# One run of products per adaLN unit, an earlier last pivot, and a buffer of its own for the gMLP gate

## The chip, the core and the metric

The kernel runs on one core of a Trainium2 chip. A core has a matrix engine (TensorE, called PE, whose weight loads are listed as PEld), a vector engine (DVE), a scalar engine (ACT), GpSimd (POOL) and a sync engine (SP) that here issues nearly all transfers, in order, to 16 DMA engines. Matrix products accumulate in PSUM, which has eight banks of 128 x 512 fp32; all else lies in SBUF. The metric is the device time of one execution in microseconds; the median of the runs is given.

## What is computed

One layer of a streaming encoder (D = 1024) is computed for two groups with the same weights: a prompt of 1024 frames and a sample of 32 rows, one for each of 32 running streams. Both have conditioning vectors `c`, from which adaLN makes six modulation vectors; three kinds of head groups share one input projection.

```python
mod = silu(c) @ w_ada + b_ada                       # 1024 -> 6 * 1024
sh1, sc1, g1, sh2, sc2, g2 = split(mod, 6)
h = x * (1 + sc1) + sh1
mq, mk, mv, mo, mi, mf, fq, fk, fv, ff, gu, gv = split(h @ w_in)
hm = mlstm(mq, mk, mv, li, lf) -> head norm * gain * sigmoid(mo)     # 4 heads of 64
hf = softmax(q k^T * scale + F_i - F_j, causal) v                    # FoX, 8 heads of 64
hg = gu * (w_s (causal, blocks of 128) @ layer_norm(gv) + b_s)       # gMLP, 4 groups of 64
x = layer_norm(ALPHA * x + (1 + g1) * (concat(hm, hf, hg) @ w_o))
h = x * (1 + sc2) + sh2
y = (silu(h @ w_gate) * (h @ w_up)) @ w_down                         # 2816 wide
x = layer_norm(ALPHA * x + (1 + g2) * y)
```

The outputs are both groups' `x` and their new caches (FoX keys, values and forget values, mLSTM states, and for the sample the normalised `gv`).

## The kernel before

**Precision and products.** Every large fp32 product is taken as three fp32r products: each operand is split in a high part (an ACT cast, name ending in `hi` or `h`) and the remainder (a subtraction on DVE or POOL, `lo` or `l`), and `gemm` issues high x high (L119), high x low (L120) and low x high (L121). `tm_unit`, whose result has frames on the partitions, does the same at L315 to L317. In all listings the name before `<-` is the result and those behind it are the operands.

**Columns.** Activations lie transposed, features on partitions. The 1056 columns are two parts: part 0 holds the first 512 frames, part 1 the rest and the sample's 32 columns. `MM[0]` cuts part 0 into two pieces of 256 columns, `MM[1]` part 1 into two of 272.

**Order.** The program is written as generators. A scheduler places each instruction on its engine's stream by a simulated timeline, by the priority of its place in the program, by dependences and by free buffers; `tc.high_priority(n)` moves what is written inside it ahead by n places. A buffer is named by pool and tag, and the last argument of `self.t` is how many copies rotate. Within an engine and on SP's queue everything runs in the order that results.

**The stages**, by the profile's times:

- 0 to 57 us: `x` is loaded, the eight adaLN units 0 to 7 (sh1, sc1) are computed, and the first feature-major projection `fm_first` runs as the operand's parts become ready.
- 57 to 150 us: values (`tm_unit` with `evac_v`) and gates.
- 150 to 370 us: the list `ORDER` says what comes in turn: `q`, `k`, `v`, `o` are projections, `f` is the first half of a FoX head, `m` an mLSTM head, and `a` one adaLN unit of the list `rest`. Results for the output projection go to DRAM (`start_dmix`).
- 370 to 408 us: gMLP. Four calls of `tm_unit` alternate between `evac_gv` (normalised `gv`, stored to DRAM as `start_dvn`) and `evac_gmlp` (the gate). `evac_gmlp` reads back `gvn` (L675), copies the gate `u` out of PSUM (L677), runs four small products with the spatial weights (L682), multiplies, and hands on to `to_mix`, which transposes, copies to a buffer `mixs` (L666) and stores it. Two feature-major units for heads 2 and 3 follow (`fm_g`, evacuated to `fm_qkh` at L399).
- 408 to 490 us: the output projection of part 0 (`wo`, products `wo_g`), its layer norm, four more feature-major units. Before `wo`, `wo_res` loads eight pieces of `x` (`mlstm_z<-xT`, a buffer that reuses the memory of the mLSTM heads) and `wo_mix` loads 16 pieces of the mixed heads (`wo_tmp<-start_dmix`, four buffers), which ACT casts (L947) and DVE subtracts (L948).
- 490 to 905 us: the second halves of the FoX heads and the other mLSTM heads are woven between the feed-forward part: six groups of hidden units (`GROUPS`), for each the `up` products (`up_g`, `L119` to `L121`, with the SiLU at L1058 to L1064) and then `down` (`dn_g`).
- 905 us to the end: the output projection and feed-forward of part 1 and the last layer norms.

**adaLN unit.** `ada(u)` makes 256 columns of the modulation: eight products of `c` (128 x 32 a slice) with 128 x 256 slices of `w_ada`. Each product has 32 result rows, placed by `k` in one of the four row quarters of a bank; the first four start the sums, the other four add to them. Then ACT copies the bank, PE transposes it (L196), DVE adds the four quarters (L198) and the bias (L204). Units 0 to 7 use the tag `araw`; the later 16 are called by `more(n)` with the tag `late`, in the PSUM tag `t`.

**Pivot.** The layer norm subtracts from every row block `z[:, m]` a common row, the mean of block `m = 0` (the pivot), before it sums squares. For part 0's last norm this stood in the fifth `down` group (`g == WOB - 1`): after `m = 0` one product with `ones8` (L891), an ACT copy (L892) and a DVE subtraction; then, for each `m` from 1, a POOL subtraction ahead of the DVE addition that evacuates the product:

```python
if pivot and m:
    self.nc.gpsimd.tensor_tensor(z[:, m, sl], z[:, m, sl], st["pv"][:, sl], ALU.subtract)   # L983
...
    self.lastz = self.nc.vector.scalar_tensor_tensor(z[:, m, x:y], ps[:, x - a:y - a], g[i], z[:, m, x:y],  # L986
```

The same stands for part 1 in its second-last `down` group. The functions as they were:

Of the kernel before, what the change touches and what calls it, by code (L numbers as in the profile page):

```python
# [15 lines left out]
P = 128  # L16
D = 1024
KT = 8
# [16 lines left out]
XB, AB = (3, 6)  # L35
HPA = 200
MLB = (1, 3, 5, 6, 7)
RESE = "pp"
ORDER = "q0 f0 q1 a f1 a q2 f2 k0 a k1p s a q3 f3 a v q4 f4 a a q5 f5 a o a m0 q6 f6 a m1 q7 a m2 f7 a m3"
ADAPOS = 4  # L40
# [27 lines left out]
class Kernel:  # L68
# [103 lines left out]
    def ada_load(self, u, pool, tag, bufs):  # L172
        self.phase = "ada"
        out = [self.t(pool, [P, 1056], F32, tag, bufs)[:, :1024] for _ in range(2)]
        for half, raw in enumerate(out):
            self.load(raw, self.d["w_ada"][u, :, half * 1024:(half + 1) * 1024])
        return out

    def ada(self, u, pool, tag, bufs, ppool, ptag, loaded=None):
        self.phase = "ada"  # L180
        nc = self.nc
        ps = self.t(ppool, [P, 512], F32, ptag)
        for half in range(2):
            if loaded:
                raw = loaded[half]
            else:
                raw = self.t(pool, [P, 1056], F32, tag, bufs)[:, :1024]
                self.load(raw, self.d["w_ada"][u, :, half * 1024:(half + 1) * 1024])
            for k in range(4):
                nc.tensor.matmul(ps[32 * k:32 * k + 32, :256], self.c32[:, 4 * half + k, :],  # L190
                                 raw[:, k * 256:(k + 1) * 256], start=half == 0, stop=half == 1)
# [113 lines left out]
    def tm_unit(self, src, ncol, evac, tiles=range(9), eng=None):  # L305
# [3 lines left out]
        for tt in tiles:  # L309
# [16 lines left out]
            else:  # L326
                tmp = self.t(self.sm, [NS, 264], F32, "tmsum", 1)
                nc.scalar.copy(tmp[:, :ncol], ps[32:64, :ncol])
                r = self.t(self.sm, [NS, 264], F32, "tmres", 1)
# [218 lines left out]
    def mlstm(self, j):  # L548
# [97 lines left out]
        sq = t([P, 4, 64], "msq")  # L646
# [25 lines left out]
    def evac_gmlp(self, tt, ps, n, bank=None):  # L672
# [3 lines left out]
        u = self.t(self.sm, [P, 256], F32, "traw", 2)  # L676
# [210 lines left out]
    def ln_pivot(self, st, z, sl):  # L887
        nc = self.nc
        ps = self.t(self.pt, [P, 512], F32, "t")
# [308 lines left out]

    def down(self, c, g, act, cuts, st=None, kept=None):
# [39 lines left out]
    def run(self):  # L1239
# [54 lines left out]
        rest = list(range(16, 20)) + list(range(8, 16)) + list(range(20, 24))  # L1294

        def more(n):
            for u in rest[:n]:
                self.ada(u, self.pl, "late", 2, self.pt, "t")
            del rest[:n]
# [49 lines left out]
        def tail_ada():  # L1349
            for u in rest:  # L1350
                self.ada(u, self.wp, "raw", RAW, self.pg, "g")

        for i in range(4):
            if i == ADAPOS:
                tail_ada()
            self.tm_unit(w2[3 + i % 2], 256, (self.evac_gv, self.evac_gmlp)[i % 2], range(4 * (i // 2), 4 + i // 2 * 5),
                         nc.gpsimd if GENG[i] else nc.vector)
        if ADAPOS == 4:
            tail_ada()
# [26 lines left out]
        for g, (j0, nj) in enumerate(GROUPS):  # L1386
# [52 lines left out]
        for g, (j0, nj) in enumerate(GROUPS):  # L1439
# [134 lines left out]
```

## Time and profile before

| what | value |
|---|---|
| median of 3 runs | 1422.57 us (1421.74 to 1427.48) |
| the profiled execution's own time | 1425.93 us |
| its span | 1424.1 us |
| mean granted TensorE clock | 0.986 |
| PE busy | 1354.6 us, 95% |
| DVE, ACT, POOL busy | 995.0, 653.3, 252.2 us |
| DMA | 233.06 MB, mean 164 GB/s |

Times in the views of the profile are microseconds from the span's start. A row of the timeline gives the start, the duration, the engine and line, the result and operands, and the shapes; a bracket behind it gives how long the engine sat idle before it and what ended that. A row of groups gives the shortest, median and longest duration in ns, and the first and last start. The granted clock is the share of TensorE's full clock that the chip gave. An fp32 product (as in `ada` and the transposes) makes two records.

### The profile page before, as it was taken

The page shows a single profiled execution, that of the slowest core. Times are in us where ns is not written, and L with a number is a line of the kernel's source. Part 1 is how long each engine was busy: PE and PEld are TensorE (multiplying, and loading weights), DVE is VectorE, ACT ScalarE, POOL GpSimd, SP SyncE. Part 2 cuts the span into 40 slices and gives each one's busy share as a digit, 9 for nine tenths or more (in the row PEclk, how much of TensorE's full clock was granted, in tenths as well). Part 3 has the DMA queues.
Part 4 walks back from the last instruction along what each step waited for, and adds up shares of the span by engine and source line. Part 5 has one row for each costly group of instructions (what it writes and reads, how often), then busy time and mean ns, then how long its engine had stood idle before and what let it go on. Part 6 is the DMA issues. An engine that isn't in the chain of part 4 may idle for free.

```text
span 1424.1 us, 25412 instructions
## 1 busy us (share of the span) xinstructions
PE 1354.6 (95%) x9435; PEld 1229.5 (86%) x9435; DVE 995.0 (70%) x2144; ACT 653.3 (46%) x1308; POOL 252.2 (18%) x290
## 2 busy tenths in 40 slices
PE   7999999899899899999999999999899999999995
PEld 4799888888899778888888877798899999999985
DVE  5548655558679757676767766577977888777766
ACT  3323244443444644545455354335654564636344
POOL 0103200032145700000000000274600000000431
PEclk9999999999999999999999999999999999999997
DMA  9764588677565464354445454555675768544221
GB/s 358 244 213 134 167 241 241 178 236 210 177 192 183 144 175 136 97 150 137 123 118 147 87 124 76 191 153 151 184 195 145 216 163 225 153 136 126 84 73 64
DMA packets 136371, 233.06 MB, mean 164 GB/s; under 512 B 22564, under 2 KB 79532, under 8 KB 136248
## 3 DMA queue, kind: packets, MB, share of 16 engines
q1 hardware_dynamic: 131080, 221.48, 51.4%
q0 software_dynamic: 5168, 9.96, 4.6%
q8 instruction: 74, 1.21, 0.3%
q14 instruction: 49, 0.40, 0.1%
HBM read 197.50 MB, written 53.81 MB: 176 GB/s over the span
## 4 chain that ended last, share of the span: by engine, by line
PE 79%; DMA 8%; DVE 7%; issue 2%; ACT 2%; POOL 1%; SPq 1%; ACTq 0%; DVEq 0%
PE up_g L119 5%; PE up_g L120 5%; PE up_g L121 5%; PE dn_g L119 4%; PE dn_g L120 4%; PE dn_g L121 4%; PE tm_g L316 3%; PE tm_g L315 3%; PE tm_g L317 3%; PE fm_g L119 2%; PE wo_g L121 2%; PE wo_g L120 2%; PE wo_g L119 2%; PE fm_g L120 2%; PE sup_g L119 2%
## 5 line engine op out<-in xcount | busy, mean ns | idle before, releaser
L119 PE MATMUL up_g<-mlstm_ah,up_whi 128*128 128x512 f32 x328 | 131.4, 401 | 2.5 <-DVE up_sil L1062 1.3
L120 PE MATMUL up_g<-mlstm_al,up_whi 128*128 128x512 f32 x328 | 130.4, 397 | 0.0
L121 PE MATMUL up_g<-mlstm_ah,up_wlo 128*128 128x512 f32 x328 | 129.8, 396 | 0.0
L315 PE MATMUL tm_g<-tm_whi,start_h1h 128*128 128x256 f32 (+1 forms) x384 | 111.4, 291 | 0.8 <-ACT tm_mixs L666 0.5
L316 PE MATMUL tm_g<-tm_wlo,start_h1h 128*128 128x256 f32 (+1 forms) x384 | 110.4, 288 | 0.0
L317 PE MATMUL tm_g<-tm_whi,start_h1l 128*128 128x256 f32 (+1 forms) x384 | 110.4, 288 | 0.0
L119 PE MATMUL fm_g<-start_h1h,fm_whi 128*128 128x256 f32 (+2 forms) x344 | 102.1, 303 | 8.2 <-DVE fm_qkl L400 5.1
L120 PE MATMUL fm_g<-start_h1l,fm_whi 128*128 128x256 f32 (+2 forms) x344 | 102.0, 297 | 0.0
L121 PE MATMUL fm_g<-start_h1h,fm_wlo 128*128 128x256 f32 (+2 forms) x344 | 101.3, 295 | 0.0
L1130 ACT CAST sup_whi<-sup_raw 128x1024 fp32r<-128x1024 f32 x54 | 56.5, 1048 | 80.9 <-PE dn_u L120 33.8
L107 ACT CAST up_whi<-up_raw 128x1024 fp32r<-128x1024 f32 x50 | 52.3, 1046 | 77.3 <-PE up_g L120 39.8
L751 ACT ACTIVATE fox_p<-fox_s,fox_fmx 128x384 f32<-128x384 f32 (+2 forms) x96 | 55.3, 580 | 59.6 <-DVE fox_fmx L744 52.7
L119 PE MATMUL dn_g<-up_acth,dn_whi 128*128 128x512 f32 (+2 forms) x200 | 75.1, 376 | 5.1 <-DVE mlstm_z L986 5.1
L782 DVE TENSOR_TENSOR fox_ptl<-fox_t,fox_pth 128x512 fp32r<-128x512 f32 (+2 forms) x88 | 51.0, 588 | 40.6 <-ACT fox_pth L781 40.1
L119 PEld LDWEIGHTS fm_g<-start_h1h,fm_whi 128*128 128x128 f32 x344 | 65.6, 192 | 14.4 <-DVE fm_qkl L400 6.0
L119 PEld LDWEIGHTS up_g<-mlstm_ah,up_whi 128*128 128x128 f32 x328 | 61.6, 188 | 17.4 <-DVE fm_qkl L400 1.8
L1131 DVE TENSOR_TENSOR sup_wlo<-sup_raw,sup_whi 128x1024 fp32r<-128x1024 f32 x54 | 67.5, 1256 | 13.0 <-ACT sup_whi L1130 12.8
L108 DVE TENSOR_TENSOR up_wlo<-up_raw,up_whi 128x1024 fp32r<-128x1024 f32 x50 | 62.2, 1244 | 19.8 <-ACT up_whi L107 19.2
L315 PEld LDWEIGHTS tm_g<-tm_whi,start_h1h 128*128 128x128 f32 x384 | 72.9, 190 | 3.1 <-issue 1.2
L316 PEld LDWEIGHTS tm_g<-tm_wlo,start_h1h 128*128 128x128 f32 x384 | 72.9, 190 | 1.9 <-issue 1.6
L120 PE MATMUL dn_g<-up_actl,dn_whi 128*128 128x512 f32 (+2 forms) x200 | 74.5, 373 | 0.0
L121 PE MATMUL dn_g<-up_acth,dn_wlo 128*128 128x512 f32 (+2 forms) x200 | 74.2, 372 | 0.0
(614 smaller groups left out, 4550.1 us busy)
## 6 DMA issues: line engine op xcount, KB each, us to landing
up_raw<-w_gu SPq DMA_DIRECT2D x50, 512.0 KB
ada_late<-w_ada SPq DMA_DIRECT2D x32, 512.0 KB
dn_raw<-w_dn SPq DMA_DIRECT2D x28, 512.0 KB
wo_raw<-w_o SPq DMA_DIRECT2D x24, 512.0 KB
sup_raw<-w_gu SPq DMA_DIRECT2D x20, 512.0 KB
start_dp<-w_gu SPq DMA_DIRECT2D x19, 512.0 KB
start_dp<-w_gu POOLq DMA_DIRECT2D x19, 512.0 KB, 6.9
sup_raw<-start_dp SPq DMA_DIRECT2D x18, 512.0 KB
```

Of the source, the lines that this page charges most:

```text
L107: nc.scalar.copy(hi[:, :w], raw[:, :w])
L108: (eng or nc.vector).tensor_tensor(lo[:, :w], raw[:, :w], f(hi[:, :w]), ALU.subtract)
L119: nc.tensor.matmul(ps, hi, xh(k), start=start and k == 0, stop=False, skip_group_check=more)
L120: nc.tensor.matmul(ps, hi, xl(k), start=False, stop=False, skip_group_check=more)
L121: nc.tensor.matmul(ps, lo, xh(k), start=False, stop=stop and k == n - 1, skip_group_check=more)
L315: nc.tensor.matmul(ps[:, :ncol], xh, hi, start=k == 0, stop=False)
L316: nc.tensor.matmul(ps[:, :ncol], xh, lo, start=False, stop=False)
L317: nc.tensor.matmul(ps[:, :ncol], xl, hi, start=False, stop=k == 7)
L751: nc.scalar.activation(pr[:, lo:hi], banks[x][:, :hi - lo], AF.Exp, bias=m, scale=-1.0 if hi == n else 1.0, accum_out=sums[:, x:x + 1])
L782: nc.vector.tensor_tensor(pl[:, :at], ps[:, :at], f(ph[:, :at]), ALU.subtract)
L1130: nc.scalar.copy(h, x)
L1131: tt(l, x, f(h), ALU.subtract)
```

## The change

Four edits. First, a unit's 1 MB of `w_ada` comes in one transfer, and its eight products are issued inside `high_priority(HPU)`; the copies of the buffers are half as many, each twice as large. Second, `ORDER` holds eight `a` instead of twelve: units 20 to 23 (the gate `g2`) are computed between the `up` units of part 0's feed-forward, in the PSUM tag `g` (three banks) of the `up` products, and `tail_ada`, which had nothing left to do, is gone. Third, a new `pivot(c)` does the whole subtraction, in pieces of 256 or 272 columns, after the fourth `down` group; the fifth has no pivot. Fourth, the gate `u` of `evac_gmlp` has two buffers `gu` of its own instead of sharing the two of `traw` with `evac_gv`; `msq` of the mLSTM head shares the buffers of `mkw`, and `tmres` is computed in place.

```diff
-XB, AB = (3, 6)
+XB, AB = (3, 3)
 HPA = 200
+HPU = 3000
-ORDER = "q0 f0 q1 a f1 a q2 f2 k0 a k1p s a q3 f3 a v q4 f4 a a q5 f5 a o a m0 q6 f6 a m1 q7 a m2 f7 a m3"
-ADAPOS = 4
+ORDER = "q0 f0 q1 a f1 a q2 f2 k0 k1p s a q3 f3 a v q4 f4 a q5 f5 o a m0 q6 f6 a m1 q7 m2 f7 a m3"
...
     def ada_load(self, u, pool, tag, bufs):
         self.phase = "ada"
-        out = [self.t(pool, [P, 1056], F32, tag, bufs)[:, :1024] for _ in range(2)]
-        for half, raw in enumerate(out):
-            self.load(raw, self.d["w_ada"][u, :, half * 1024:(half + 1) * 1024])
-        return out
+        raw = self.t(pool, [P, 2048], F32, tag, bufs)
+        self.load(raw, self.d["w_ada"][u])
+        return raw
...
         ps = self.t(ppool, [P, 512], F32, ptag)
-        for half in range(2):
-            if loaded:
-                raw = loaded[half]
-            else:
-                raw = self.t(pool, [P, 1056], F32, tag, bufs)[:, :1024]
-                self.load(raw, self.d["w_ada"][u, :, half * 1024:(half + 1) * 1024])
-            for k in range(4):
-                nc.tensor.matmul(ps[32 * k:32 * k + 32, :256], self.c32[:, 4 * half + k, :],
-                                 raw[:, k * 256:(k + 1) * 256], start=half == 0, stop=half == 1)
+        with self.tc.high_priority(HPU):
+            for k in range(KT):
+                r = slice(32 * (k % 4), 32 * (k % 4) + 32)
+                nc.tensor.matmul(ps[r, :256], self.c32[:, k, :], raw[:, k * 256:(k + 1) * 256],
+                                 start=k < 4, stop=k >= 4)
...
-                r = self.t(self.sm, [NS, 264], F32, "tmres", 1)
+                r = tmp
...
-        sq = t([P, 4, 64], "msq")
+        sq = t([P, 4, 64], "mkw")
...
-        u = self.t(self.sm, [P, 256], F32, "traw", 2)
+        u = self.t(self.sm, [P, 256], F32, "gu", 2)
...
-    def ln_pivot(self, st, z, sl):
+    def ln_pivot(self, st, z, sl, pool=None, tag="t"):
         nc = self.nc
-        ps = self.t(self.pt, [P, 512], F32, "t")
+        ps = self.t(pool or self.pt, [P, 512], F32, tag)
...
+    def pivot(self, c):
+        st = self.ln_begin(self.nc.gpsimd, early=True)
+        st["pivot"] = False
+        self.phase = f"dn{c}"
+        for a, b in MM[c]:
+            self.ln_pivot(st, self.z[c], slice(a, b), self.pg, "g")
+            for m in range(1, KT):
+                z = self.z[c][:, m, a:b]
+                st["eng"].tensor_tensor(z, z, st["pv"][:, a:b], ALU.subtract)
+        return st
...
-        rest = list(range(16, 20)) + list(range(8, 16)) + list(range(20, 24))
+        rest = list(range(16, 20)) + list(range(8, 16))
...
-                self.ada(u, self.pl, "late", 2, self.pt, "t")
+                self.ada(u, self.pl, "late", 1, self.pt, "t")
...
                 weave(self.up(0, j, act, pa, FC[0]))
-            if g == WOB - 1:
-                st = self.ln_begin(nc.gpsimd, early=True)
-                self.down(0, g, act, FC[0], st)
-            else:
-                self.down(0, g, act, FC[0])
-        st.update(pivot=False)
+                if j < 4:
+                    self.ada(20 + j, pa, "late", 1, self.pg, "g")
+            self.down(0, g, act, FC[0])
+            if g == WOB - 2:
+                st = self.pivot(0)
...
             if g < last:
-                st = self.ln_begin(nc.gpsimd, early=True) if g == last - 1 else None
-                self.down(1, g, act, MM[1], st)
-        st.update(pivot=False, order=(4, 5, 6, 7, 0, 1, 2, 3))
+                self.down(1, g, act, MM[1])
+            if g == last - 2:
+                st = self.pivot(1)
+        st.update(order=(4, 5, 6, 7, 0, 1, 2, 3))
```

The edits also change the scheduler's order. PE, in the head: before, the fourth adaLN unit of the head has its products in two pieces of four (`ada_t_328`); the numbers behind names tell buffers apart.

```order
L119 MATMUL fm_g_185<-start_h1h_168,fm_whi_248 128x512
L190 MATMUL ada_t_328<-ada_araw_323,start_c_63_181 32x256 x4
L120 MATMUL fm_g_186<-start_h1l_171,fm_whi_248 128x272
L121 MATMUL fm_g_186<-start_h1h_170,fm_wlo_249 128x272
L120 MATMUL fm_s_187<-start_h1l_171,fm_whi_248 128x272
```

After, the same unit (`ada_t_320`, the line is now L186) has them in one:

```order
L119 MATMUL fm_g_185<-start_h1h_168,fm_whi_244 128x512
L186 MATMUL ada_t_320<-ada_araw_316,start_c_63_181 32x256 x8
L120 MATMUL fm_g_186<-start_h1l_171,fm_whi_244 128x272
L121 MATMUL fm_g_186<-start_h1h_170,fm_wlo_245 128x272
L120 MATMUL fm_s_187<-start_h1l_171,fm_whi_244 128x272
```

All 24 units stand so: 24 pieces of eight, where before there were 40 pieces.

ACT, just before the output projection of part 0. Before, the casts of the mixed heads (L947) are spread among the gMLP copies (L666, L677) and the feature-major evacuations (L399):

```order
L947 CAST mlstm_ah_4416<-wo_tmp_4430 128x256
L666 COPY tm_mixs_5171<-tm_g_5132 128x256
L677 COPY tm_traw_5239<-tm_tmres_5235 32x256
L947 CAST mlstm_ah_4416<-wo_tmp_4434 128x256
L947 CAST mlstm_ah_4416<-wo_tmp_4438 128x256
L947 CAST mlstm_ah_4416<-wo_tmp_4442 128x256
L947 CAST mlstm_ah_4416<-wo_tmp_4446 128x256
L947 CAST mlstm_ah_4416<-wo_tmp_4450 128x256
L399 ACTIVATE fm_qkh_5285<-fm_g_5260,start_qsc_146 128x272
```

After, all gMLP copies come first (the gate's is now L673 and the mixed result's L662), and twelve of the sixteen casts (now L943) stand behind the last feature-major evacuation (now L395):

```order
L943 CAST mlstm_ah_4284<-wo_tmp_4298 128x256
L107 CAST wo_whi_5377<-wo_raw_5375 128x1024
L395 ACTIVATE fm_qkh_5260<-fm_g_5235,start_qsc_146 128x272
L943 CAST mlstm_ah_4284<-wo_tmp_4302 128x256
L943 CAST mlstm_ah_4284<-wo_tmp_4306 128x256
L943 CAST mlstm_ah_4284<-wo_tmp_4310 128x256
L943 CAST mlstm_ah_4284<-wo_tmp_4314 128x256
L943 CAST mlstm_ah_4284<-wo_tmp_4318 128x256
```

On SP the loads of `x` for part 0 (`mlstm_z<-xT`) stood ahead of the last gMLP stores; now they stand behind nearly all of them, and still behind the store of the last mLSTM head:

```order
L90 DMA start_dmix_32_88<-mlstm_mixs_4261 128x2x128
L90 DMA start_dmix_33_89<-tm_mixs_5038 128x2x128
L86 DMA wo_raw_5412<-w_o 128x1024
L86 DMA mlstm_z_834_4275<-xT 128x512 x8
L86 DMA wo_tmp_4286<-start_dmix_32_88 128x256
```

On PE, 177 products stood between that head's transposes and the first `wo_g`; now there are 108.

PE, at part 0's last pivot. Before, it stands between the last FoX products and the fifth `down` group:

```order
L789 MATMUL fox_o_8366<-fox_pth_8393,fox_v_8164 128x256
L891 MATMUL dn_t_10312<-mlstm_z_878_4407,start_ones_45_139 128x512
L784 MATMUL fox_o_8366<-fox_ptl_8407,fox_v_8164 64x256
L789 MATMUL fox_o_8366<-fox_pth_8406,fox_v_8164 128x256
L784 MATMUL fox_o_8366<-fox_ptl_8407,fox_v_8164 64x256
L789 MATMUL fox_o_8366<-fox_pth_8406,fox_v_8164 128x256
L119 MATMUL dn_g_10373<-up_acth_9795,dn_whi_10369 128x512
```

After, it stands in two pieces (now L887) between the fourth `down` group and `up` products, and the last FoX products stand within the fifth `down` group:

```order
L121 MATMUL dn_g_9935<-up_acth_9669,dn_wlo_9918 128x512
L887 MATMUL dn_g_9950<-mlstm_z_834_4275,start_ones_45_139 128x256
L737 MATMUL fox_s_7914<-fox_k_1544_7763,fox_qp_7764 128x384
L738 MATMUL fox_s_7914<-fox_k_1546_7765,fox_q_1547_7766 128x384
L887 MATMUL dn_g_9961<-mlstm_z_834_4275,start_ones_45_139 128x256
L119 MATMUL up_g_9986<-mlstm_ah_4284,up_whi_9976 128x512
```

POOL's seven subtractions of 128 x 512 become fourteen of 128 x 256, all behind the fourth group.

More of the change, by code (lines that the diff above doesn't have):

```diff
@@ L173, in ada_load @@
         self.phase = "ada"
-        out = [self.t(pool, [P, 1056], F32, tag, bufs)[:, :1024] for _ in range(2)]
-        for half, raw in enumerate(out):
-            self.load(raw, self.d["w_ada"][u, :, half * 1024:(half + 1) * 1024])
-        return out
+        raw = self.t(pool, [P, 2048], F32, tag, bufs)
+        self.load(raw, self.d["w_ada"][u])
+        return raw
     def ada(self, u, pool, tag, bufs, ppool, ptag, loaded=None):
+        raw = loaded if loaded is not None else self.ada_load(u, pool, tag, bufs)
         self.phase = "ada"
@@ L1348, in run @@
         self.wo_mix(0, self.KORDER[:6])
-        def tail_ada():
-            for u in rest:
-                self.ada(u, self.wp, "raw", RAW, self.pg, "g")
         for i in range(4):
-            if i == ADAPOS:
-                tail_ada()
             self.tm_unit(w2[3 + i % 2], 256, (self.evac_gv, self.evac_gmlp)[i % 2], range(4 * (i // 2), 4 + i // 2 * 5),
                          nc.gpsimd if GENG[i] else nc.vector)
-        if ADAPOS == 4:
-            tail_ada()
         for h in range(QD, PRE):
```

## The prediction, before the result was known

> **What bounds the kernel now.** I read the page's busy times and span first, then the share of the chain of waits by engine.
>
> ```profile
> span 1424.1 us, 25412 instructions
> PE 1354.6 (95%) x9435; PEld 1229.5 (86%) x9435; DVE 995.0 (70%) x2144; ACT 653.3 (46%) x1308; POOL 252.2 (18%) x290
> ...
> PE   7999999899899899999999999999899999999995
> ...
> PE 79%; DMA 8%; DVE 7%; issue 2%; ACT 2%; POOL 1%; SPq 1%; ACTq 0%; DVEq 0%
> ```
>
> TensorE (PE) is busy for 95% of the span and carries 79% of the chain that ends last. The row of digits is PE's busy share in tenths, in 40 slices of 35.6 us. The time changes in three ways only: PE does less work, PE waits less or more, or the granted clock changes. The second reading is therefore the table by stretches of time, for those that the diff touches (columns: microseconds, then busy time of PE, PEld, DVE, ACT, POOL, the granted clock, the DMA share, GB/s).
>
> ```profile
> 0.00:50.00 50.00, 37.51 (x260) 23.37 (x261) 27.54 (x82) 16.24 (x35) 6.27 (x20) 0.97 0.87 324
> 15.00:20.00 5.00, 5.00 (x40) 2.72 (x38) 0.27 (x2) 0.37 (x1) 0.00 (x0) 1.00 1.03 413
> ...
> 350.00:400.00 50.00, 44.51 (x351) 42.12 (x351) 34.53 (x119) 22.03 (x62) 9.03 (x12) 0.93 0.57 179
> 389.00:393.00 4.00, 3.30 (x18) 3.04 (x19) 1.87 (x9) 1.11 (x4) 0.00 (x0) 0.50 0.88 270
> 393.00:397.00 4.00, 4.00 (x24) 4.00 (x24) 2.01 (x8) 1.12 (x3) 0.00 (x0) 0.68 0.75 228
> ...
> 894.00:898.00 4.00, 2.14 (x8) 1.78 (x9) 2.18 (x4) 0.53 (x2) 4.00 (x4) 0.92 0.27 64
> 898.00:902.00 4.00, 4.00 (x13) 3.08 (x13) 1.05 (x2) 0.42 (x1) 4.00 (x4) 0.65 0.95 320
> ```
>
> Three places have something to give: the head (PE 37.5 of 50 us), the end of the projections at 350 to 400 (44.5 of 50, clock 0.93), and the pivot at 894 to 902 (clock 0.65 behind a gap).
>
> **Part 1, adaLN products in one run.** PE runs the products of a unit between those of a projection; each product makes two records. Start, duration and count, around a run of four and a run of eight:
>
> ```profile
> 68.42 0.28 PE L316 MATMUL tm_g<-tm_wlo,start_h1h 128*128 128x264 f32 x1
> 68.63 0.64 PE L190 MATMUL ada_t<-ada_late,start_c 128*32 128x256 f32 x8
> 69.20 0.39 PE L317 MATMUL tm_g<-tm_whi,start_h1l 128*128 128x264 f32 x1
> 69.43 0.29 PE L315 MATMUL tm_g<-tm_whi,start_h1h 128*128 128x264 f32 x1
> 69.55 0.28 PE L316 MATMUL tm_g<-tm_wlo,start_h1h 128*128 128x264 f32 x1
> ...
> 81.96 1.07 PE L190 MATMUL ada_t<-ada_late,start_c 128*32 128x256 f32 x16
> 82.96 0.39 PE L315 MATMUL tm_g<-tm_whi,start_h1h 128*128 128x264 f32 x1
> ...
> L190 PE MATMUL ada_t<-ada_late,start_c x256: 379/379/404, 68.6 to 367.4; 128*32 128x256 f32 x128
> ```
>
> From start to start, neighbouring 264-column products are 0.125 us apart (69.43 to 69.55), but the run is entered after 0.21 (68.42 to 68.63) and left after 0.23 (69.20 to 69.43): 0.09 and 0.10 extra. Four products take 0.57, eight take 1.00. A unit split in two runs costs 2 x 0.57 − 1.00 + 0.19 = 0.33 us more than one in a single run. The trace has 40 runs, 13 for the eight units of the head and 27 for the sixteen later ones; the changed order has 24. So 16 x 0.33 = 5.3 us, 1.7 of them in the head. The head's share is uncertain, because PE waits there anyway, so the bounds are −3 and −6; I take −5.3, the larger end, because most runs lie where PE is full.
>
> The transfer of 1 MB: every one of the 256 late records stands in the trace without a wait for its transfer, and in the changed order the load has its buffer some 7 us ahead or more, since at least 56 products of 0.125 lie between the buffer's release and its next use. I cost it at nothing; cover gone, a unit waits at most one transfer of the head's kind, and that is this row:
>
> ```profile
> 3.78 8.31 DMA ada_araw<-w_ada
> ```
>
> Twenty-four fewer issues on SP cost and gain nothing, since SP is 1% of the chain. In the head the DMA moves 413 GB/s at 15 to 20 us with the 512 KB transfers, so longer ones have nothing to raise there: 0. The Trainium skill ("DMA: Bandwidth & Descriptors", the rule under its bandwidth figures) says to batch transfers to 1 MiB or more; for 1 MiB its figure is 341 GB/s, against the 324 of the head's row, so 50 us would become 47.5 by an estimate, and the sum 2.5 more negative. The row of 413 GB/s, reached with 512 KB, speaks against it.
>
> Four units move from 200 to 370 us to between the up products at 490 to 560. PE's digits are 8 and 9 in both stretches, so their work moves and saves nothing: 0. There they take one of three PSUM banks that the up products rotate through, and the next up group waits until an earlier bank is read. The rows of one such wait and of what reads a bank:
>
> ```profile
> 510.13 0.48 PE L119 MATMUL up_g<-mlstm_ah,up_whi 128*128 128x512 f32 x1 [1.26 <-DVE up_sil L1062]
> ...
> L1058 ACT ACTIVATE up_sil<-up_g x3: 588/591/594, 496.7 to 516.7; 128x512 f32<-128x512 f32 x3
> L1059 ACT ACTIVATE up_sil<-up_sil,start_ones x3: 712/722/724, 497.3 to 517.3; 128x512 f32<-128x512 f32 x3
> L1060 ACT ACTIVATE up_sil<-up_sil x3: 627/630/632, 498.9 to 518.1; 128x512 f32<-128x512 f32 x3
> L1061 DVE TENSOR_TENSOR up_sil<-up_g,up_sil x2: 684/688/692, 502.3 to 512.1; 128x512 f32<-128x512 f32 x2
> ```
>
> A whole chain is 0.59 + 0.72 + 0.63 + 0.69 = 2.6 us, while an up group of 24 products takes 4.8: a 128x512 product takes 0.2, by the 13 records in the 4 us of 898 to 902 at a clock of 0.65. So mostly the reader is done in time. Bounds 0 and four times 4.5 (the chain and its queue); I take one wait like the 1.26: +1.3.
>
> **Part 2, the gMLP gate in own buffers.** The rows run from the last mLSTM head's transposes to the stop of PE (start, duration; the bracket is the idle time before and what ended it).
>
> ```profile
> 375.21 0.38 PE L664 MATMUL mlstm_t<-start_ident,mlstm_mhm 128*128 128x128 f32 x2
> 377.83 3.81 SPq L86 DMA_DIRECT2D mlstm_z<-xT  x8
> 385.15 3.75 DMA start_dmix<-tm_mixs
> 389.00 0.37 ACT tm_mixs L666
> 389.70 2.93 PE L682 MATMUL tm_g<-tm_gvn,start_wsp 128*128 128x64 f32 x16 [3.94 <-ACT tm_traw L677]
> 398.60 0.39 PE L119 MATMUL fm_g<-start_h1h,fm_whi 128*128 128x272 f32 x1 [0.97 <-ACT tm_mixs L666]
> ```
>
> SP issues the eight xT loads, and the store of a gMLP result stands behind them and lands at 388.9; only then is its buffer free for the ACT copy L666, and the gate's copy L677 is queued behind that. PE waits 3.94 and later 0.97, and the clock is half in between. From 389 to 393 the clock is 0.50, and 0.68 over the next four us means 0.50 up to 395.6. From 389.70, where PE starts again, that is 5.9 us at half, a loss of 2.95. With the gate's own buffers the gMLP tiles stand ahead of the last mLSTM head on all engines, and their stores ahead of the xT loads. The whole goes: −(3.94 + 0.97) − 2.95 = −7.9, at worst one us stays.
>
> **What is late next.** The same move takes the cover from the output projection. Before, 177 products lie between the last mLSTM head's transposes and the first product `wo_g`; now 108, and the loads of the mixed heads (`wo_tmp`) still wait for that head and stand behind xT on SP.
>
> ```profile
> L86 SPq DMA_DIRECT2D wo_tmp<-start_dmix x16: 319/386/1839, 381.7 to 403.6; - x16
> L947 ACT CAST mlstm_ah<-wo_tmp x16: 392/405/422, 387.4 to 405.8; 128x256 fp32r<-128x256 f32 x16
> ...
> 407.76 0.28 PE L119 MATMUL wo_g<-mlstm_ah,wo_whi 128*128 128x256 f32 x1
> ```
>
> From the xT issue (377.83) to the first cast (387.4) it takes 9.6 us; the sixteen casts go in four groups of four buffers, 18.4 us from first to last, so 4.6 a group. Counted from the transposes T0: xT at T0 + 2.6, first cast at T0 + 12.2, the fourth group at T0 + 26, and its first two casts feed the eighteen-product first accumulation. PE now reaches those at about T0 + 17: 108 products at 0.125 make 13.5, with some 1.5 for starting and small ones, and 2 for the part of the first accumulation that earlier casts feed. I take a wait of 9 us, in one or two pieces, and one half-clock stretch behind it, priced below at 1.7: +10.7. Bounds: by the casts alone twelve stand behind the last fm evacuation, of 0.41 us each, less what PE still has to do: +3; with the whole 31 us that passed before from T0 to the last cast, +14. Zero only if xT came earlier.
>
> **Part 3, the pivot.** It stands in the fifth down group now, where PE goes straight on.
>
> ```profile
> 888.48 0.38 PE L784 MATMUL fox_o<-fox_ptl,fox_v 128*128 128x256 f32 x1 [2.09 <-DVE fox_ptl L782]
> 891.00 0.33 PE L784 MATMUL fox_o<-fox_ptl,fox_v 128*64 128x256 f32 x1 [0.49 <-DVE fox_ptl L782]
> 891.53 1.02 PE L891 MATMUL dn_t<-mlstm_z,start_ones 128*128 128x512 f32 x2
> 893.25 9.21 POOL L983 TENSOR_TENSOR mlstm_z<-mlstm_z,up_pv 128x512 f32<-128x512 f32 x7 [58.20 <-ACT up_pv L892]
> 895.86 0.50 PE L119 MATMUL dn_g<-up_acth,dn_whi 128*128 128x512 f32 x1 [2.84 <-DVE mlstm_z L986]
> ```
>
> The waits of 2.09, 0.49 and 2.84 are followed by a half clock that costs 4 x 0.35 + 4 x 0.08 = 1.7 by the two rows of 894 to 902: 7.1 together. After the change the subtractions run beside an up group, and the fox tail's products stand between those of the down group. I leave 1.0 for fox waits that stay: −6.1; bounds −7.1 and −3 (if the fox waits of 2.58 stay). POOL does 14 smaller subtractions for 7; for that size there is:
>
> ```profile
> L386 POOL TENSOR_TENSOR tm_traw<-tm_traw,start_rowp x9: 727/735/741, 307.6 to 373.6; 128x256 f32<-128x256 f32 x8, 32x256 f32<-32x256 f32 x1
> ```
>
> 14 x 0.735 = 10.3 us beside the up products of four units, 192 x 0.2 = 38 us: 0. The Trainium skill ("TensorE: Matmul & The Clock Gate", its table of goals) allows idle gaps up to about 3 us before the clock halves; by it the 2.84 would have cost no clock, and the sum would be 1.7 less negative. The row of 898 to 902 shows 0.65 behind that gap, so the row decides. The sample's pivot had no PE gap and gains 0.
>
> **The sum.** −5.3 + 1.3 − 7.9 + 10.7 − 6.1 = −7.3 us. The profiled execution gives 1425.93, 0.24% over the median of the runs, 1422.57; from the median the forecast is 1415.
>
> **Rivals.** (a) The output projection waits 3 us, as the casts alone say, with no half clock: −15, so 1408. For it: loads may leave earlier when SP has fewer issues ahead of them; against it: xT still waits for the last mLSTM head. (b) The gains are eaten: a wait of 14 and its clock (+15.7), and fox waits that stay (−3 instead of −6.1): +0.8, so 1420 to 1423. The 31 us of the trace speak for it. (c) Slower: the four units hold a bank of three while PE works through 17 to 40 rows, and each up group then waits the whole chain, 4.5 us, with 1.7 of clock: 4 x 6.2 = 25 less 8.6 for the rest, so 1439. It turns to slower than before above about 2 us a unit. Against it: a bank is read in 2.6 us. (d) The longer transfers raise the head's mean of 324 GB/s to the 413 of its best stretch: its 16.2 MB take 39 us, so 11 less and 1404. Against it: with 512 KB the DMA's share is already 1.03 there, and PE's own 37.5 us leave little room.
>
> **How the numbers follow.** Forecast (1409 to 1419) 0.45, (a) 0.22, (b) 0.20, (c) 0.09, (d) 0.04. About 0.5%, here 7.1 us, is what a measurement of this kernel can tell from no change, so faster means below 1415.5. Half of the forecast's cases and nearly all of (a) and (d) lie there: 0.48; the other half and (b) lie within: 0.43; slower is (c), 0.09. The range from 1403 to 1424 holds the forecast, (a), (b) and (d), and leaves out (c) and the far ends of (a) and (b).
>
> **What would show it.** Right: 24 runs of ada products, each of 16 records; no wait of PE for L673 or L662 copies near 385 to 395; a wait of some 9 us before or just behind the first `wo_g`, ended by `mlstm_ah` or `mlstm_al`, with a half clock; no gap at the pivot, with PE going from `fox_o` to `dn_g`. Wrong: PE waits for a w_ada transfer, or for up_sil more than once a unit at 490 to 560, or the wait at `wo_g` is under 4 or over 13 us.

## The result, and the profile after

The changed kernel takes 1411.81 us (median of 4 runs, 1403.45 to 1414.3), the kernel before 1424.61 in the runs beside it; the ratio is 0.990 with a 95% interval of 0.9852 to 0.9947, so 0.5 to 1.5% faster. The forecast was 1415, 7.6 us less than the median then known; measured are 12.8 less. The profiled execution took 1411.39. These are the lines of its page that answer to those of before (span, busy times, PE's forty slices, the chain of waits):

```profile
span 1409.6 us, 25370 instructions
PE 1346.1 (95%) x9437; PEld 1229.6 (87%) x9437; DVE 999.4 (71%) x2145; ACT 656.3 (47%) x1309; POOL 261.1 (19%) x297
PE   6999999999989899999999999999989999999995
PE 73%; DMA 10%; DVE 8%; ACT 3%; issue 3%; POOL 2%; SPq 1%; ACTq 0%; DVEq 0%; POOLq 0%
```

PE is still busy for 95%, with 8.5 us less work. The page doesn't say where the time went, so the span is cut into stages at the first product of each kind. First four stages of before, then the same of after (columns as in the prediction: stretch, length, busy time of PE, PEld, DVE, ACT, POOL, clock, DMA share, GB/s): value projections, projections and mixers up to the first `wo_g`, output projection of part 0 up to the first `up_g`, and the fifth group up to the output projection of part 1.

```profile
54.78:122.41 67.63, 67.63 (x569) 65.54 (x567) 35.12 (x106) 15.85 (x32) 3.36 (x4) 1.00 0.68 225
122.41:407.76 285.35, 267.34 (x2176) 245.22 (x2174) 179.68 (x549) 111.17 (x284) 54.94 (x74) 0.98 0.67 199
407.76:483.59 75.83, 73.07 (x590) 72.31 (x589) 66.88 (x108) 43.08 (x79) 50.14 (x47) 1.00 0.55 171
812.37:919.89 107.52, 100.84 (x478) 80.33 (x477) 66.13 (x131) 47.93 (x97) 10.14 (x8) 0.98 0.51 118
```

```profile
51.63:118.95 67.32, 67.32 (x568) 65.66 (x567) 35.53 (x107) 15.96 (x32) 3.37 (x4) 1.00 0.66 223
118.95:381.46 262.51, 253.18 (x2104) 240.30 (x2102) 173.20 (x517) 105.25 (x266) 56.09 (x73) 0.99 0.64 191
381.46:467.50 86.04, 76.03 (x590) 74.09 (x589) 73.50 (x126) 48.56 (x94) 51.83 (x47) 0.98 0.59 182
805.11:902.96 97.85, 96.12 (x469) 77.40 (x468) 62.48 (x116) 43.73 (x86) 12.72 (x15) 1.00 0.48 116
```

The second stage is 22.8 us shorter, the output projection of part 0 is 10.2 longer, and the fifth group is 9.7 shorter. In the output projection PE idles 10.0 us (86.04 − 76.03) where it idled 2.8. The view of what PE waited for from 380 to 480 us (total, times, longest) names the cause:

```profile
PE wo_g L119 <- ACT mlstm_ah L943: 4.9, 1, 4.9
PE fm_g L119 <- DVE fm_qkl L396: 2.9, 2, 1.4
PE up_g L119 <- DVE fm_qkl L396: 2.5, 1, 2.5
PE wo_g L119 <- DVE mlstm_z L982: 0.7, 1, 0.7
PE wo_g L119 <- DVE fm_qkl L396: 0.7, 1, 0.7
```

The forecast wait for the mixed heads is there (4.9), with three of 0.7 around it. The 2.9 of `fm_g` stood there before too (2.8), and the 2.5 of `up_g`, at 473.0 us, lies just behind this stage. So 7.2 of the 10.2 us are new idle time, and 3.0 are longer busy time for the same products, at a clock of 0.98. At the last gMLP tiles a stop of 0.5 us is left.

The table gives the length of every stage, from the rows of such views of the kernels below (us; one profiled execution each). Such an execution can lie some us from the median of its kernel: that of the pivot alone, 1422.07, is the fastest of twelve.

| stage, up to the first | before | after | edit 1 alone | pivot alone | after, gate in `traw` | after, late pivot | after, units in `ORDER` |
|---|---|---|---|---|---|---|---|
| value projection | 54.8 | 51.6 | 52.2 | 54.0 | 51.8 | 51.3 | 51.6 |
| gate product | 67.6 | 67.3 | 67.3 | 67.6 | 67.3 | 67.3 | 67.3 |
| `wo_g`, part 0 | 285.4 | 262.5 | 274.4 | 284.8 | 272.8 | 261.8 | 274.3 |
| `up_g` | 75.8 | 86.0 | 77.0 | 76.0 | 76.0 | 87.2 | 85.8 |
| second `up` group | 81.1 | 90.7 | 79.6 | 79.5 | 90.0 | 88.8 | 77.4 |
| fifth `up` group | 247.7 | 246.9 | 247.7 | 249.9 | 246.9 | 245.9 | 249.8 |
| `wo_g`, part 1 | 107.5 | 97.9 | 107.2 | 97.9 | 98.3 | 104.1 | 97.7 |
| `up`, part 1's start | 49.0 | 50.1 | 49.0 | 56.5 | 50.5 | 49.0 | 55.8 |
| last layer norm | 422.5 | 423.9 | 421.1 | 422.2 | 421.4 | 421.8 | 418.7 |

### The profile page after: what moved, and what is told of

It reads as the page before. It is cut to its first block, busy times and chain, and to the rows that moved or that the text cites. A ratio compares the mean times of both kernels' runs of the same rounds, so it can differ in the third digit from the quotient of the medians.

```text
span 1409.6 us, 25370 instructions
## 1 busy us (share of the span) xinstructions
PE 1346.1 (95%) x9437; PEld 1229.6 (87%) x9437; DVE 999.4 (71%) x2145; ACT 656.3 (47%) x1309; POOL 261.1 (19%) x297
## 3 DMA queue, kind: packets, MB, share of 16 engines
q1 hardware_dynamic: 127624, 221.48, 51.3%
## 4 chain that ended last, share of the span: by engine, by line
PE 73%; DMA 10%; DVE 8%; ACT 3%; issue 3%; POOL 2%; SPq 1%; ACTq 0%; DVEq 0%; POOLq 0%
PE up_g L121 4%; PE up_g L119 4%; PE up_g L120 4%; PE dn_g L119 4%; PE dn_g L120 4%; PE dn_g L121 4%; PE tm_g L312 2%; PE tm_g L313 2%; PE tm_g L311 2%; PE fm_g L119 2%; PE sup_g L119 2%; PE sup_g L121 2%; PE sup_g L120 2%; PE fm_g L120 2%; PE fox_t L773 2%
## 5 line engine op out<-in xcount | busy, mean ns | idle before, releaser
L1126 ACT CAST sup_whi<-sup_raw 128x1024 fp32r<-128x1024 f32 x54 | 56.5, 1048 | 78.3 <-PE dn_u L120 37.2
L120 PEld LDWEIGHTS up_g<-mlstm_al,up_whi 128*128 128x128 f32 x328 | 62.1, 189 | 14.1 <-issue 0.8
L121 PEld LDWEIGHTS up_g<-mlstm_ah,up_wlo 128*128 128x128 f32 x328 | 62.1, 189 | 13.9 <-issue 0.4
L313 PEld LDWEIGHTS tm_g<-tm_whi,start_h1l 128*128 128x128 f32 x384 | 73.0, 190 | 0.6 <-issue 0.4
```

The lines of the kernel that those rows point to most:

```text
L120: nc.tensor.matmul(ps, hi, xl(k), start=False, stop=False, skip_group_check=more)
L121: nc.tensor.matmul(ps, lo, xh(k), start=False, stop=stop and k == n - 1, skip_group_check=more)
L313: nc.tensor.matmul(ps[:, :ncol], xl, hi, start=False, stop=k == 7)
L1126: nc.scalar.copy(h, x)
```

## The experiments

**One edit at a time on the kernel before.** Edit 1 alone:

```diff
-XB, AB = (3, 6)
+XB, AB = (3, 3)
+HPU = 3000
...
-        out = [self.t(pool, [P, 1056], F32, tag, bufs)[:, :1024] for _ in range(2)]
+        raw = self.t(pool, [P, 2048], F32, tag, bufs)
...
+        with self.tc.high_priority(HPU):
+            for k in range(KT):
...
```

> The kernel before with one transfer and one run of eight products per adaLN unit alone (ORDER, gate buffers and pivot as before). Theory of the runs: 24 runs instead of 40 at 0.33 us each, -5.3 us in all, of which 1.7 to 3.2 by the start of the first value projection (54.8 us before), and about -3.5 more by 370 us; the pivot gap at 888 to 896 stays. Rival, the parts of the time gained before 370 us belong to the four units that left: then this kernel stands at -3.5 us at 109 us and gains no more until the output projection. Since the order also puts the gMLP tiles differently around the last mLSTM head (157 products from its transposes to the output projection, 176 before), the stop at 389 us may be smaller by some us; a whole of -4 to -9 us against before.

Measured: 1411.54 us (7 runs), ratio 0.9927 (0.9893 to 0.9961), 10 us faster by the ratio, and at the level of the whole change. The price of a run is confirmed where nothing else happens, in the value projections, where the clock is 1.00 and PE never idles. The stage of this kernel:

```profile
52.24:119.56 67.32, 67.32 (x569) 65.66 (x567) 35.57 (x107) 15.95 (x32) 3.36 (x4) 1.00 0.67 222
```

Two units lie there, three runs before and two now, and the stage is 67.32 instead of 67.63: 0.31 us for a run, forecast 0.33. In every kernel here with two runs in that stage it is 67.3, in those with three 67.6. The rival falls: this kernel reaches the output projection 13.8 us before the old one with all units still in `ORDER`. The stop of 3.94 us at the gMLP tiles is 1.62 in its trace, and the load of `gvn` ends it instead of the gate's copy:

```profile
382.31 0.63 PE L679 MATMUL tm_g<-tm_gvn,start_wsp 32*32 32x64 f32 x8 [1.62 <-DMA tm_gvn<-start_dvn]
```

So that stop shrinks without the gate's own buffers, but does not go whole; a half clock still follows it (0.66 from 384 to 388 us).

The gate's buffers alone:

```diff
-        u = self.t(self.sm, [P, 256], F32, "traw", 2)
+        u = self.t(self.sm, [P, 256], F32, "gu", 2)
```

> The kernel before with the gate's own buffers (and msq, tmres shared) alone. Theory of the store: the stop of 3.94 us at 389.7 comes from the gMLP store that waits on the sync engine behind the eight xT loads, not from the sharing of traw; the order still has gMLP tiles behind the last mLSTM head (47 products behind its transposes), so a stop of 2 to 4 us and its half clock stay before the output projection, 0 to -3 us in all. Rival, the shared buffer is the cause: the stop goes whole, -5 to -8 us before the output projection, and 3 to 6 us come back as a wait for the mixed heads.

Measured: 1426.39 (12 runs), 1.0012 (0.9989 to 1.0035). The stop is gone, as the rival said, but waits in the mixers before it took its place (the first `wo_g` starts at 407.94, before at 407.76), and this came back at the output projection:

```profile
418.04 0.62 PE L119 MATMUL wo_g<-mlstm_ah,wo_whi 128*128 128x256 f32 x3 [3.46 <-ACT mlstm_ah L947]
```

The earlier pivot alone:

```diff
...
+            self.down(0, g, act, FC[0])
+            if g == WOB - 2:
+                st = self.pivot(0)
...
```

> The kernel before with the earlier pivot alone. Theory: nothing changes before the fourth down group ends (772 to 812 us), and the stretch from the last up group (872.7) to the end of the fifth down group (908.9), 36.1 us before, is 7 to 10 us shorter, with no idle time between fox_o and dn_g; for part 1 another 1 to 2 us at 1006. -7 to -10 us in all. Rival: the gain there belongs to the fox work that the other edits moved, and the pivot alone gives at most the 2.84 us gap and its half clock, -3 to -4.5 us.

Measured: 1427.68 (12 runs), 1.0016 (0.9993 to 1.0039): no gain. The stretch is 9.7 us shorter, as the theory said, but 7.4 are lost in the next stage, and the stage ahead of it is 2.2 longer. The two stages of this kernel, and what PE waits for in the second:

```profile
811.64:909.50 97.86, 96.31 (x468) 77.63 (x468) 65.78 (x122) 43.45 (x86) 12.17 (x15) 1.00 0.47 100
909.50:965.96 56.46, 52.75 (x390) 51.59 (x389) 37.63 (x59) 19.50 (x38) 27.44 (x30) 0.94 0.68 197
...
PE wo_g L119 <- ACT up_ah L947: 3.0, 2, 1.9
PE wo_t L891 <- DVE wo_z L986: 0.7, 1, 0.7
```

`up_ah` is the mixed heads of part 1. The last `fox_o` and the first `wo_g` of part 1 in this kernel, and then in the changed one:

```profile
899.35 0.28 PE L789 MATMUL fox_o<-fox_pth,fox_v 128*128 128x256 f32 x1
909.50 0.29 PE L119 MATMUL wo_g<-up_ah,wo_whi 128*128 128x272 f32 x1
```

```profile
887.24 0.28 PE L785 MATMUL fox_o<-fox_pth,fox_v 128*128 128x256 f32 x1
902.96 0.29 PE L119 MATMUL wo_g<-up_ah,wo_whi 128*128 128x272 f32 x1
```

With 10.2 us between them PE waits 3.7 and the clock takes 3.4 more (56.46 x 0.06); with 15.7 it waits 0.2 there. In the kernel before, 27.2 us lay between the two (892.74 to 919.89): there the fifth `down` group stood behind the last FoX products and covered the way of their result through DRAM.

Moving the four units alone:

```diff
...
+                if j < 4:
+                    self.ada(20 + j, pa, "late", 2, self.pg, "g")
```

> The kernel before with units 20 to 23 moved between the up units of part 0 alone (two transfers and split runs as before, two buffers). Theory: the four units take 1.6 us each out of the stretch up to 370 us and add the same plus 0.5 to 1 us each between 490 and 560 us, so +2 to +4 us at 625 us against what is gained earlier; whole time within 3 us of before, or +2 to +4 when the gMLP stop stays. Rival: the units' PE work was in the way of nothing and the move itself is worth some of the -12.8 us of the whole change: -3 us or more.

Measured: 1415.3 (12 runs), 0.9937 (0.9917 to 0.9957). The rival was right in sign: 9 us faster, though the move takes no work away. The mean granted clock of its runs is 0.989 against 0.986: 0.0037 x 1420, so some 5 of the 9 us, is clock. In its trace the gMLP stop is 2.90 instead of 3.94, again with the load of `gvn` at its end:

```profile
382.62 0.63 PE L682 MATMUL tm_g<-tm_gvn,start_wsp 32*32 32x64 f32 x8 [2.90 <-DMA tm_gvn<-start_dvn]
```

**One edit undone in the changed kernel.** Edit 1 undone (two transfers, products in two loops):

> The changed kernel with edit 1 undone: two transfers a unit and products as the scheduler puts them (39 runs). Theory of stages: the 15 runs more cost 5 us, 2 to 3 of them by the first value projection (51.6 us in the changed kernel), the rest stays as in the changed kernel, so -7.5 us against before (-0.5%). Rival, the edits add up as their single runs did (-0.73, +0.12, +0.16 and -0.63%): -0.27%, -4 us.

Measured: 1420.71 (12 runs), 0.9969 (0.9954 to 0.9983). The single effects add up to this better than my stages did: edit 1 is worth 8.9 us within the change (1420.71 − 1411.81), of which 15 runs at 0.31 make 4.7. The two profiled executions are 11.2 us apart: 4.7 for the runs, 3.0 of idle time and some 3.5 of busy time beyond the runs. Most of the idle time, 2.8 us, is at part 0's output projection, where the wait for the mixed heads is 8.5 us in all instead of 4.9:

```profile
PE wo_g L119 <- ACT mlstm_ah L947: 8.5, 2, 6.8
```

The gate back in `traw`:

> The changed kernel with the gMLP gate back in traw (msq and tmres in their own buffers again). Theory of stages: 169 products lie between the last mLSTM head's transposes and the output projection instead of 107, so the wait of 4.9 us for the mixed heads and its half clock go, and a stop of PE at the last gMLP tiles of 0 to 4 us may come back in its place: -13 to -20 us against before. Rival, the buffers are needed for the whole gain: the stop of 3.9 us and its half clock come back whole with nothing gained behind it, -5 us. By adding single effects: -1.12%, -16 us.

Measured: 1409.64 (5 runs), 0.9898 (0.9876 to 0.992): as fast as the whole change. The stages to the first `wo_g` and from there to `up_g`:

```profile
119.13:391.96 272.83, 255.01 (x2103) 240.39 (x2102) 178.53 (x531) 108.95 (x278) 55.70 (x74) 0.99 0.63 191
391.96:467.92 75.96, 73.17 (x591) 72.41 (x590) 67.93 (x111) 43.84 (x81) 51.46 (x47) 1.00 0.58 180
```

Against the changed kernel's 262.51 and 86.04 the buffers bring 10.3 us before the output projection, and 10.1 come back in it.

The pivot back in the fifth group:

> The changed kernel with the pivot back in the fifth down group. Theory of stages: the pivot is worth the 9.4 us that the stretch from the last up group to the end of part 1's output projection lost in the changed kernel (93.4 to 86.9 us there, against 96.3 before), because there the last FoX products end 15 us before part 1's output projection and nothing waits for them: without it -3.4 us against before (-0.25%), with the two gaps of 2.1 and 2.6 to 2.8 us back. Rival, the pivot is worth nothing, as its single run says (+0.16%): -1.16%, -16 us.

Measured: 1412.79 (5 runs), 0.9914 (0.9893 to 0.9935). The stretch is 6.2 us longer, with the wait for `mlstm_z` of 2.8 back, but the next two are 1.1 and 2.1 shorter. Timed, the pivot is worth 1 us within the change, which the intervals don't tell from 0. My 9.4 was wrong: it compared with the kernel before, whose fox work stands otherwise.

Units 20 to 23 back in `ORDER`:

> The changed kernel with units 20 to 23 back in ORDER. Theory of stages: before 370 us it is 6.4 us later, and by 625 us 3.3 us earlier, because the up products don't share banks with the units; but in the order the last FoX products stand only 44 products ahead of part 1's output projection, as in the kernel with the pivot alone (68 in the changed kernel), so PE waits there for the mixed heads and 6 to 9 us come back: -8 us against before (-0.55%), with waits of wo_g for up_ah of 2 to 4 us in all and a half clock behind. Rival, the move is needed for the whole gain only as far as its single run says: -0.37%, -5 us, without a wait there.

Measured: 1414.12 (6 runs), 0.9929 (0.9905 to 0.9953), 10 us less than before, with the expected wait. The stage of part 1's output projection and its waits:

```profile
903.90:959.73 55.83, 52.56 (x390) 51.41 (x388) 38.17 (x59) 19.46 (x38) 27.43 (x30) 0.94 0.70 199
...
PE wo_g L119 <- ACT up_ah L943: 2.5, 2, 1.4
PE wo_t L887 <- DVE wo_z L982: 0.7, 1, 0.7
```

The same order there as with the pivot alone gives about the same loss, 6.8 us and 7.4. So what the move does in that stage is to bring the last FoX products forward, to 15.7 us ahead of the first `wo_g` instead of 10.2; over the whole, its 2.3 us (1414.12 − 1411.81) are not told from 0.

**The wait at part 0's output projection.** Loads of `x` issued by GpSimd:

```diff
-            self.load(z[:, k], self.d["xT"][k, :, GO[c]:GO[c] + GN[c]])
+            self.nc.gpsimd.dma_start(z[:, k], self.d["xT"][k, :, GO[c]:GO[c] + GN[c]])
```

> The changed kernel with the eight loads of x for part 0 issued by GpSimd instead of the sync engine; PE's order is the same. Theory of the queue: the loads of the mixed heads stand 4.94 us of issue time behind those eight loads; freed of them each of their four groups starts up to 4.9 us earlier, so the wait of 4.92 us at the output projection and its half clock of 1.7 us go: -5 to -9 us against the changed kernel, -18 to -22 us (-1.3 to -1.5%) against before. Rival, the cycle of four buffers and the casts sets the end: the first group comes earlier, the last not, and 0 to -2 us are gained on the changed kernel.

Measured: 1409.29 (6 runs), 0.9887 (0.9862 to 0.9912). Issues on SP and the wait, first in the changed kernel, then here:

```profile
370.71 4.94 SPq L86 DMA_DIRECT2D mlstm_z<-xT  x8
375.89 2.31 SPq L86 DMA_DIRECT2D wo_tmp<-start_dmix  x4
391.45 1.98 SPq L86 DMA_DIRECT2D wo_tmp<-start_dmix  x4
...
394.34 1.01 PE L119 MATMUL wo_g<-mlstm_ah,wo_whi 128*128 128x256 f32 x3 [4.92 <-ACT mlstm_ah L943]
```

```profile
370.30 2.53 SPq L86 DMA_DIRECT2D wo_tmp<-start_dmix  x4
390.28 1.50 SPq L86 DMA_DIRECT2D wo_tmp<-start_dmix  x3
...
393.71 1.01 PE L119 MATMUL wo_g<-mlstm_ah,wo_whi 128*128 128x256 f32 x3 [4.74 <-ACT mlstm_ah L943]
```

The first group leaves 5.6 us earlier and the last loads 1.2; the wait stays. The rival is right: what counts is the last group, which stands behind the stores of the feature-major units. The 2.5 us against the changed kernel are not told from 0.

Loads of the mixed heads written ahead of `x`:

```diff
-        self.wo_res(0, self.pz)
         self.operand(0, self.ph)
         self.wo_mix(0, self.KORDER[:6])
+        self.wo_res(0, self.pz)
```

> The changed kernel with the loads of the mixed heads written ahead of the loads of x; both stay on the sync engine, and the order puts four loads of the mixed heads, three of x, four, five of x, four, then the stores, and four more; PE's order is the same. Theory of the queue: the last group still stands behind all eight loads of x, but the stores of the feature-major units now stand behind the third group; the wait shrinks by the 2 to 3 us that those stores took between the groups, -2 to -5 us against the changed kernel. Rival, the first group's late start is what counts: -5 to -9 us as with the loads on GpSimd.

Measured: 1406.96 (5 runs), 0.987 (0.9845 to 0.9896), 4.9 us below the changed kernel, the size that the first theory gave, but not by its way: the last group still leaves at 390.7, and the wait has another end.

```profile
387.48 0.58 PE L119 MATMUL wo_g<-mlstm_ah,wo_whi 128*128 128x256 f32 x1 [4.64 <-DVE fm_qkl L396]
```

PE waits for a PSUM bank that `fm_qkl` has to evacuate on DVE. That instruction stands behind four subtractions that waited 1.82 us for their casts, and then waits 0.63 us itself for the store of an earlier `fm_qkl`. Of the 5.1 us between the two profiled spans' starts of the last layer norm, 2.0 are in this stage; the rest is clock and small waits elsewhere.

The last group also ahead of the last feature-major units:

```diff
+        self.wo_mix(0, self.KORDER[6:])
         for h in range(QD, PRE):
             self.fm_unit(w3[2 + h], self.evac_qk(h), (1,))
         s6.close()
-        self.wo_mix(0, self.KORDER[6:])
```

> The kernel with the loads of the mixed heads ahead of x (the run before this one), with the fourth group of them (gMLP's part of the mixed heads) also written ahead of the last two feature-major units; PE's products stand as before but for one pivot product. On the sync engine the fourth group stands behind five stores of the feature-major units instead of twelve or more. Theory of the queue: that group, issued at 390.7 us there, leaves some 5 us earlier, so the sums of part 0's output projection no longer wait for it; but the wait of 4.6 us at the first wo_g for the evacuation fm_qkl, whose DVE instruction stands behind subtractions that wait for a load, may stay: -1 to -4 us against the run before, -1.4 to -1.6% against the kernel before. Rival, the vector engine's order sets the end and not the loads: the last fm_qkl now stands behind the fourth group's subtractions and the wait grows to 6 us or more: +1 to +4 us against the run before.

Measured: 1408.68 (6 runs), 0.9851 (0.9819 to 0.9883). The two are not told apart (1406.96 and 1408.68). The wait is 5.49 now, for the same evacuation: it grows as the rival said, though not to its 6:

```profile
392.96 0.58 PE L119 MATMUL wo_g<-mlstm_ah,wo_whi 128*128 128x256 f32 x1 [5.49 <-DVE fm_qkl L396]
```

Both beat the kernel before; against the changed kernel the intervals of both overlap its own. Moving the evacuations ahead on DVE wasn't tried.

**Transfer or priority.** The changed kernel without the priority (`HPU = 0`):

> The changed kernel with HPU = 0: one transfer of 1 MB a unit, but no priority for its products, which the order now splits into 37 runs (24 with the priority). Theory of the runs: it loses what the kernel with edit 1 undone lost, 13 runs x 0.33 = 4.3 us and the idle time and half clocks that went with them, so -0.3% against before, within 3 us of that kernel (1420.7). Rival, the transfer of 1 MB brings the gain: it stays at -1.0%.

Measured: 1416.22 (8 runs), 0.9937 (0.9915 to 0.9959). It loses 4.4 us, about the 13 runs (13 x 0.31 = 4.0), but its interval and the changed kernel's overlap, and its profile (1420.88, the slowest of the eight) does not put the loss at the runs. Nine of the 13 lie ahead of the first `wo_g`, which starts only 1.5 us later (382.97). The output projection is 3.6 us longer, with a wait of 6.2 for the mixed heads, and an `up` product waits for a bank that a unit holds:

```profile
492.61 0.79 PE L119 MATMUL up_g<-mlstm_ah,up_whi 128*128 128x512 f32 x1 [3.23 <-DVE ada_adam L194]
```

So that the transfer alone doesn't bring the gain is likely, but not shown. This kernel is 4.5 us better than the one with edit 1 undone, with two runs fewer; whether the transfer of 1 MB or the order gives that is open. The priority with two transfers was not run.

## Why the prediction came out as it did

- **Part 1, −5.3: right in its price, too small in its size.** All 24 units stand in one run, at 0.31 us a run saved. Within the change the edit is worth 8.9; idle time, most of it the wait for the mixed heads (8.5 against 4.9), and half clocks went along with the runs, which the term left out.
- **Transfers of 1 MB: 0, held.** No late unit waits for one. In the head the first unit starts at 6.8 us instead of 5.5, and its next wait is 2.2 us, for a cast, where it was 3.1 for a transfer; no gain is seen there beyond the five runs saved (1.6) and a half clock (1.6). The half clock isn't the transfer's: the kernel with the move alone, with two transfers, has a clock of 1.00 there as well.
- **The bank, +1.3: wrong place.** The `up` products waited 0.4 us for a bank held by a unit; without the priority such a wait was 3.23. What was late instead is the `up_g` at 473.0 us, 2.52 us for `fm_qkl` (0.88 before), with a half clock behind.
- **Part 2, −7.9, and what is late next, +10.7: the exchange was right, the cause only in part.** The trade is −10.3 and +10.1 by the kernel with the gate in `traw`. With its own buffers alone the stop goes whole, as forecast. But edit 1 alone and the move alone cut it too, to 1.62 and 2.90, with the load of `gvn` at its end: how long it is hangs on the order of gMLP tiles, stores and loads as well as on the buffer. The wait came as 4.9 and three of 0.7, not as 9 in one or two pieces.
- **Part 3, −6.1: the failed step.** The gap closed as forecast (9.7 us shorter), but I never asked what is late next there, which I did ask of part 2. Alone the edit gives 0, because the mixed heads of part 1 are late; within the change it gives 1 us, not told from 0.
- **The move, 0: too small.** Alone it gives 9 us, some 5 of them clock; within the change 2.3 (1414.12 − 1411.81, with overlapping intervals).

So −7.3 against −12.8: a mis-sized edit 1 (3.6 more), an unpriced move, and a pivot that gives less than its term. That the time still lies within the forecast's 1409 to 1419 is in part luck: edit 1 and the move gave 3.6 and 2.3 more than priced, the pivot 5.1 less. The measured gain lies nearer to rival (a), −15, whose wait of 3 us is also nearer to the 4.9; but with its smaller waits and the clock that stage lost the 10.2 us of the forecast, and the rest came from elsewhere.

## What to carry to other kernels

Where one engine is the bound and waits in order, closing a gap moves products, and a transfer that they had covered becomes the wait: for each gap that an edit closes, look for the load that leaves behind the same producer, and count the time from it to its first use. A stop that shrinks, or ends on something else, with any of three unrelated edits belongs to the order as much as to the buffer named beside it; only undoing one edit at a time in the changed kernel tells what each is worth.

## What the runs showed of the hardware

The half clock came after waits well under its own length. The wait of 1.93 us at 140 us in the changed kernel is followed by clocks of 0.50 and 0.70; the same wait in the kernel before (1.89) is not:

```profile
140.27 0.39 PE L119 MATMUL fm_g<-start_h1h,fm_whi 128*128 128x256 f32 x1 [1.93 <-DVE fm_qkl L396]
...
142.00:144.00 2.00, 2.00 (x12) 2.00 (x11) 1.97 (x2) 0.76 (x3) 2.00 (x3) 0.50 0.41 117
144.00:146.00 2.00, 2.00 (x14) 2.00 (x14) 1.97 (x3) 0.38 (x1) 1.88 (x4) 0.70 0.05 12
```

```profile
143.71 0.39 PE L119 MATMUL fm_g<-start_h1h,fm_whi 128*128 128x256 f32 x1 [1.89 <-DVE fm_qkl L400]
...
144.00:146.00 2.00, 2.00 (x19) 2.00 (x19) 1.90 (x4) 1.72 (x3) 1.33 (x3) 1.00 0.34 108
```

All 14 kernels here have this wait, of 1.89 to 1.93 us, in the one execution of each that was profiled. In three of them (the changed kernel, edit 1 alone and `HPU = 0`) the mean clock from 136 to 150 us is 0.88, in the other eleven 1.00. So a wait of some 2 us costs a further 1.7 in some executions and nothing in others, and differences of that size between two rows of the stage table can be chance. This is much of the spread between runs of one kernel: of the changed kernel, the run of 1403.45 had a mean clock of 0.991, the other three 0.985 or 0.986, and 0.005 x 1405 is 7 of the 8 to 11 us between them. The Trainium skill ("TensorE: Matmul & The Clock Gate", Part 1) says that the clock is set by a window of about 3.4 us that runs freely. This agrees with the same wait having two outcomes. Its table of goals, which allows gaps up to about 3 us, does not agree with the 1.93.
